# A four-layer decoder trunk on one core: x and result in whole quarters, a reordered norm chain, and eight weight parts split ahead of a layer

## The chip, the cores and the metric

The kernel runs on one core of one Trainium2 chip. The metric is the device time of one execution in microseconds; the median of several runs is given. Beside the runs there is one profiled execution with its trace. TensorE is PE in the profile, VectorE is DVE, ScalarE is ACT, GpSimd is POOL and SyncE is SP.

## The reference

256 tokens of 1024 values pass through four residual layers, and then one last RMSNorm. Layers 0 and 3 are a causal pooling mixer, layer 1 is a gated DeltaNet, layer 2 is latent attention. All is float32.

```python
def rmsnorm(x, g):
    xf = x.astype(jnp.float32)
    y = xf * lax.rsqrt(jnp.mean(xf * xf, axis=-1, keepdims=True) + EPS)
    return (y * g.astype(jnp.float32)).astype(x.dtype)

def reference(x, ...):
    for i in range(DEPTH):
        kind, j = i % N_MIXERS, i // N_MIXERS
        h = rmsnorm(x, norm_g[i])
        if kind == 0:
            y = pool_mixer(h, ...)
        elif kind == 1:
            y = gdn_mixer(h, ...)
        else:
            y = mla_mixer(h, ...)
        x = x + y.astype(x.dtype)
    return rmsnorm(x, final_g)
```

Every mixer is one wide input projection of `h`, work inside the mixer, and one output projection back to 1024 values.

## The kernel before, in words

**Layout.** The 256 tokens are two tiles of 128 partitions (`xs[0]`, `xs[1]`, called tile 0 and tile 1). Partition b*64 + a holds token 2a + b of its tile: `by_row` writes the DRAM side as a view with the order b, a, c. A tile is loaded and stored in quarters: quarter (t, c) is tile t, columns 512c to 512c + 511. Each `xs` tile has one extra column, `D`.

**Products in three parts.** A float32 product is made of three passes. Each operand is split into a high part, rounded to the matmul format (`hi`), and the rest (`lo`). For a weight, ACT casts `hi` (tile `whi`, line 149 or 153) and DVE, for some parts POOL, subtracts to get `lo` (tile `wlo`, line 150 or 154). A weight part is 128 rows of 512 columns; `weights` loads two parts (a unit) with one transfer on SP's queue into a `raw` buffer, and splits both. The split parts live in a ring of nine buffers each. A strip is 512 output columns, that is eight parts where the input has 1024 values.

**A layer's end.** `layer_out` makes the output projection in two strips of 512 columns. The second strip holds its last three units (six parts) back and then finishes the four pieces (tile 0 or 1, 256 columns each) in turn. `done` adds each piece to x on DVE (line 450) and calls `part_done`, which keeps a running sum of squares: ACT sums the squares (`sumsq`, line 256), POOL adds it to what came before. After the third quarter of the columns POOL puts a square root into the extra column of x (lines 297 and 298), so that the last sum of squares, over 257 columns, already holds the earlier ones. POOL then raises it to the power -1/2 (`xr`, line 390). `Normed.begin` multiplies 256 columns by the gain ahead of time on POOL (`hg`, line 385), and `rest` makes the two halves of the normed `h`: 256 columns of each on DVE (line 397), 256 on ACT from `hg` (line 402). PE transposes `h` (line 417) and ACT and DVE split it (lines 242 and 247) into `hT`, with which the next layer's first strip begins (line 162 for all weight matmuls).

**Order.** Each engine runs its instructions in one fixed order, which a scheduler writes from its own model of time when the kernel is built. `later(...)` tells it to keep an instruction behind a given one of the same engine. `held_back` uses this at the seam between two layers: the first `FREE` weight parts of the next layer may be split whenever the scheduler likes, and all further ones go behind the split of tile 0's `hT`:

```python
            held = held_back["free"] <= 0
            held_back["free"] -= 1
            with later(*(held_back["after"] if held else ())):
```

**Beginning and end.** At the start the quarters of x are loaded on SP's queue between the first weights (`load_x`, line 307; two transfers of 64 partitions per quarter). At the end `Final.feed` norms a tile and stores it with four transfers of 64 partitions on SP's queue (line 442). The tile pool `s4` holds the larger tiles of all layers (4 KB per partition each).

## Time and profile before

| | |
|---|---|
| median of the runs | 828.32 us (827.48 to 829.5, 3 runs) |
| profiled execution | 832.1 us, its span 830.4 us |
| granted TensorE clock | 0.986 of full speed, mean |
| PE, PEld busy | 96%, 91% of the span |
| DVE, ACT, POOL busy | 73%, 59%, 19% |
| transfers | 139.90 MB, mean 168 GB/s |

Times in the views count from the first instruction. A row of the timeline gives the start, the length, the engine, the line, the operation with output and inputs, and in square brackets how long the engine was idle before it and which instruction ended that idle time. PEld is the weight load of a matmul, which runs beside matmuls.

### The profile page before, as it was taken

What the parts mean: (1) busy time and instruction counts of PE and PEld (TensorE: products, weight loads), DVE (VectorE), ACT (ScalarE), POOL (GpSimd) and SP (SyncE); (2) the same over time, 40 slices, a digit from 0 to 9 for tenths busy, and PEclk for the clock granted to TensorE, in tenths of its full rate; (3) what the DMA queues carried; (4) which work ended last, traced back from release to release, by engine and by line L of the source; (5) the groups of instructions that cost most, each with busy time, mean ns of one, the idle gap of its engine ahead of it and who ended that gap; (6) DMA issues with size and microseconds to landing.
All of it is one profiled execution on the core that took longest, in us unless ns stands there. A gap on an engine that the chain in (4) does not pass through costs nothing.

```text
span 830.4 us, 16162 instructions
## 1 busy us (share of the span) xinstructions
PE 799.4 (96%) x5966; PEld 758.0 (91%) x5966; DVE 603.4 (73%) x1141; ACT 492.9 (59%) x993; POOL 159.8 (19%) x296
## 2 busy tenths in 40 slices
PE   8989999999898979999999999999999999999996
PEld 7989988989898978788989999999999989999996
DVE  4699887666987967356666678778877767877772
ACT  6665565567855655255566564666665565566662
POOL 2001100334236992023121112000000120000012
PEclk9999999999999989899999999999999999999998
DMA  6865666756655544303647786653552547576662
GB/s 204 224 180 167 193 209 210 221 153 195 193 135 180 163 139 118 124 12 115 187 125 224 231 180 185 192 164 102 153 175 80 179 143 214 183 223 202 202 204 51
DMA packets 109079, 139.90 MB, mean 168 GB/s; under 512 B 21316, under 2 KB 51208, under 8 KB 109000
## 3 DMA queue, kind: packets, MB, share of 16 engines
q1 hardware_dynamic: 106608, 137.12, 55.0%
q0 software_dynamic: 528, 1.58, 0.6%
q8 instruction: 47, 0.77, 0.4%
q10 hardware_dynamic: 1864, 0.17, 0.2%
q14 instruction: 32, 0.26, 0.1%
HBM read 137.27 MB, written 1.58 MB: 167 GB/s over the span
## 4 chain that ended last, share of the span: by engine, by line
PE 67%; DVE 11%; POOL 8%; DMA 8%; issue 4%; ACT 2%; SPq 0%; POOLq 0%; DVEq 0%; ACTq 0%
PE acc L162 53%; PE aux L162 7%; POOL pr L846 3%; DVE wlo L154 3%; POOL Tb L850 2%; DMA raw<-in_pool_w_out_dram 2%; DVE wlo L150 1%; DMA raw<-in_pool_w_in_dram 1%; DVE win L551 1%; DMA T<-d_t 1%; DMA Lb<-d_l 1%; DVE h L397 1%; DMA Gb<-d_g 1%; PE aux L979 1%; PE tp L1314 1%
## 5 line engine op out<-in xcount | busy, mean ns | idle before, releaser
L150 DVE TENSOR_TENSOR wlo<-raw,whi 128x512 fp32r<-128x512 f32 (+1 forms) x366 | 254.2, 719 | 104.3 <-ACT whi L149 100.8
L149 ACT CAST whi<-raw 128x512 fp32r<-128x512 f32 (+1 forms) x380 | 223.7, 617 | 167.6 <-PE acc L162 82.3
L162 PE MATMUL acc<-hTh,whi 128*128 128x256 f32 x832 | 230.7, 278 | 2.3 <-ACT gsg L670 1.5
L162 PE MATMUL acc<-hTl,whi 128*128 128x256 f32 x832 | 231.2, 278 | 0.0
L162 PE MATMUL acc<-hTh,wlo 128*128 128x256 f32 x832 | 229.8, 277 | 0.0
L162 PEld LDWEIGHTS acc<-hTh,whi 128*128 128x128 f32 x832 | 160.7, 193 | 2.9 <-ACT gsg L670 1.7
L162 PEld LDWEIGHTS acc<-hTl,whi 128*128 128x128 f32 x832 | 160.8, 193 | 0.3
L162 PEld LDWEIGHTS acc<-hTh,wlo 128*128 128x128 f32 x832 | 160.7, 193 | 0.1
L162 PE MATMUL acc<-wlo,yTh 128*128 128x256 f32 (+1 forms) x384 | 112.7, 312 | 0.8 <-DVE wlo L154 0.8
L162 PE MATMUL acc<-whi,yTh 128*128 128x256 f32 (+1 forms) x384 | 112.3, 315 | 0.0
L162 PE MATMUL acc<-whi,yTl 128*128 128x256 f32 (+1 forms) x384 | 89.1, 313 | 0.0
L162 PEld LDWEIGHTS acc<-wlo,yTh 128*128 128x128 f32 x384 | 73.2, 191 | 4.8 <-DVE wlo L154 1.7
L162 PEld LDWEIGHTS acc<-whi,yTh 128*128 128x128 f32 x384 | 72.9, 191 | 3.1
L162 PEld LDWEIGHTS acc<-whi,yTl 128*128 128x128 f32 x384 | 63.1, 191 | 3.4
L154 DVE SCALAR_TENSOR_TENSOR wlo<-raw,colsT,whi 128x512 fp32r<-128x512 f32 x64 | 47.0, 769 | 21.1 <-ACT whi L153 20.7
L153 ACT ACTIVATE whi<-raw,gain 128x512 fp32r<-128x512 f32 x64 | 43.6, 720 | 31.1 <-DMA raw<-in_pool_w_in_dram 22.6
L153 ACT ACTIVATE whi<-raw,colsT 128x512 fp32r<-128x512 f32 x64 | 43.5, 720 | 30.9 <-DMA raw<-in_pool_w_out_dram 18.0
L385 POOL TENSOR_TENSOR hg<-x,gain 128x256 f32<-128x256 f32 x16 | 13.4, 850 | 244.1 <-DVE x L450 244.1
L162 PE MATMUL acc<-wlo,hTh 128*128 128x512 f32 (+1 forms) x144 | 54.8, 385 | 1.9 <-DVE wlo L150 1.3
L154 DVE SCALAR_TENSOR_TENSOR wlo<-raw,gain,whi 128x512 fp32r<-128x512 f32 x64 | 46.6, 748 | 11.1 <-ACT whi L153 11.1
L162 PE MATMUL acc<-whi,hTh 128*128 128x512 f32 (+1 forms) x144 | 52.7, 379 | 0.7 <-ACT hTh L242 0.7
L162 PE MATMUL acc<-whi,hTl 128*128 128x512 f32 (+1 forms) x144 | 42.5, 373 | 0.0
(364 smaller groups left out, 1530.9 us busy)
## 6 DMA issues: line engine op xcount, KB each, us to landing
raw<-in_pool_w_in_dram SPq DMA_DIRECT2D x62, 512.0 KB, 4.4
raw<-in_gdn_w_in_dram SPq DMA_DIRECT2D x48, 512.0 KB, 4.0
raw<-in_pool_w_out_dram SPq DMA_DIRECT2D x32, 512.0 KB, 4.4
raw<-in_mla_w_in_dram SPq DMA_DIRECT2D x24, 512.0 KB, 4.5
raw<-in_mla_w_uq_dram SPq DMA_DIRECT2D x36, 256.0 KB, 3.4
raw<-in_pool_w_grp_dram SPq DMA_DIRECT2D x16, 512.0 KB, 3.8
raw<-in_gdn_w_out_dram SPq DMA_DIRECT2D x16, 512.0 KB, 3.8
raw<-in_mla_w_ukv_dram SPq DMA_DIRECT2D x32, 256.0 KB, 3.3
```

What stands on the lines that cost most here:

```text
L149: a = nc.scalar.copy(hi, v)
L150: b = e.tensor_tensor(out=lo, in0=v, in1=hi.bitcast(F32), op=ALU.subtract)
L153: a = nc.scalar.activation(hi, v, AF.Copy, scale=g)
L154: b = e.scalar_tensor_tensor(out=lo, in0=v, scalar=g, in1=hi.bitcast(F32), op0=ALU.mult, op1=ALU.subtract)
L162: return nc.tensor.matmul(inorder(o, n), lhsT=lhs, rhs=woven(rhs, n), start=start, stop=stop)
L385: nc.gpsimd.tensor_tensor(out=self.early[t, a], in0=xs[t][:, sl], in1=self.g[:, sl], op=ALU.mult)
L397: nc.vector.scalar_tensor_tensor(out=h[:, cut:], in0=xs[t][:, sl], scalar=r[:, 0:1], in1=self.g[:, sl], op0=ALU.mult, op1=ALU.mult)
L551: nc.vector.tensor_tensor(out=nxt[:, :, d:], in0=cur[:, :, d:], in1=cur[:, :, :S - d], op=ALU.add)
L846: nc.gpsimd.tensor_tensor(out=pv, op=ALU.mult, in0=Lb[:, r, r + 1:, None].to_broadcast([M * Q, n, c]), in1=Tb[:, r:r + 1, :c].to_broadcast ...
L850: mark["blocks"] = nc.gpsimd.tensor_tensor(out=tv, in0=tv, in1=pv, op=ALU.subtract).ins
L979: nc.tensor.matmul(ps[:, c], lhsT=U[0][:, h, :], rhs=vR[h // 2][:, 0, c * DV:(c + 1) * DV], start=True, stop=True)
L1314: nc.tensor.transpose(ps[:, a * P:(a + 1) * P], sb[:, a * P:(a + 1) * P], ident)
```

## The change

Four edits.

1. `load_x` and `Final.feed` move a quarter with one transfer instead of two. The last quarter of tile 1 is stored from ACT's queue.
2. `part_done` leaves out the division by `D` for the first three pieces of columns, so that POOL's multiplication ahead of the square root falls away; the small constant is scaled to fit.
3. `begin` for the columns from 512 on, which was free to run earlier on POOL, goes behind the square root (`mark["sofar"]`).
4. `FREE` is 8 instead of 4. Of the eight parts, the first four take ring buffers and the last four (`SPARE`) take a tile `wx` each from the pool `s4`, which holds high and low part together.

```diff
-    FREE = 4
+    FREE = 8
+    SPARE = 4
...
-            lo = ring.tile([P, CW], F32R, tag="wlo", name="wlo")[:, :cols]
-            hi = ring.tile([P, CW], F32R, tag="whi", name="whi")[:, :cols]
+            if 0 < held_back["free"] <= SPARE:
+                both = big("wx", 2, CW, dt=F32R)
+                hi, lo = both[:, 0, :cols], both[:, 1, :cols]
+            else:
+                lo = ring.tile([P, CW], F32R, tag="wlo", name="wlo")[:, :cols]
+                hi = ring.tile([P, CW], F32R, tag="whi", name="whi")[:, :cols]
...
+        unit = 1.0 / D if end or apart else 1.0
         with later(*[m for e, m in mark.items() if e == "rest"]):
-            sumsq(xs[t][:, a:a + n + more], n + more, s, scale=float(D) ** -0.5)
+            sumsq(xs[t][:, a:a + n + more], n + more, s, scale=unit ** 0.5)
         if a == 0:
-            nc.gpsimd.tensor_scalar(s, s, EPS, None, ALU.add)
+            nc.gpsimd.tensor_scalar(s, s, EPS * D * unit, None, ALU.add)
...
         if a and not end:
-            nc.gpsimd.tensor_scalar(s, s, float(D), None, ALU.mult)
-            nc.gpsimd.tensor_tensor(out=xs[t][:, D:], in0=s, in1=half, op=ALU.pow)
+            mark["sofar"] = nc.gpsimd.tensor_tensor(out=xs[t][:, D:], in0=s, in1=half,
+                                                    op=ALU.pow).ins
...
-        for b in range(2):
-            nc.sync.dma_start(out=xs[t][b * 64:(b + 1) * 64, sl], in_=by_row(x, t)[b, :, sl])
+        nc.sync.dma_start(out=xs[t][:, sl], in_=by_row(x, t)[:, :, sl])
...
-                for b in range(2):
-                    nc.sync.dma_start(out=by_row(out, t)[b, :, sl],
-                                      in_=y[c][b * 64:(b + 1) * 64])
+                queue = nc.scalar if c and t == NT - 1 else nc.sync
+                queue.dma_start(out=by_row(out, t)[:, :, sl], in_=y[c])
...
             if c == 0:
-                nxt.begin(t, CW)
+                with later(mark.pop("sofar")):
+                    nxt.begin(t, CW)
```

## The prediction

> **What bounds the kernel now.** I read the page's busy times first, then the chain of work that ended last, then the timeline at the start, at each seam between two layers, and at the end.

> ```profile
> span 830.4 us, 16162 instructions
> PE 799.4 (96%) x5966; PEld 758.0 (91%) x5966; DVE 603.4 (73%) x1141; ACT 492.9 (59%) x993; POOL 159.8 (19%) x296
> PE 67%; DVE 11%; POOL 8%; DMA 8%; issue 4%; ACT 2%; SPq 0%; POOLq 0%; DVEq 0%; ACTq 0%
> ```

> TensorE is busy for 96% of the span and carries 67% of the chain. The change touches none of its matmuls, so it can only win the idle time of PE (31 us in all) in the places that it touches, and the stretches before PE starts and after it ends. Those places are the loads of x, the three seams where a layer's last strip meets the next layer's first strip, and the tail. At the seams PE's own rows say what it waits for:

> ```profile
> 172.49 0.48 PE L162 MATMUL acc<-wlo,hTh 128*128 128x512 f32 x1 [0.65 <-POOL wlo L150]
> 173.38 0.48 PE L162 MATMUL acc<-wlo,hTh 128*128 128x512 f32 x1 [0.18 <-DVE wlo L150]
> 423.38 0.48 PE L162 MATMUL acc<-whi,hTh 128*128 128x512 f32 x1 [0.24 <-ACT hTh L242]
> 427.02 0.48 PE L162 MATMUL acc<-wlo,hTh 128*128 128x512 f32 x1 [0.57 <-DVE wlo L150]
> 674.53 0.48 PE L162 MATMUL acc<-wlo,hTh 128*128 128x512 f32 x1 [0.53 <-DVE wlo L150]
> 423.20:430.00 6.80, 6.05 (x31) 5.02 (x32) 5.78 (x10) 5.60 (x13) 1.03 (x2) 1.00 0.46 117
> ```

> The bracket is PE's idle time before the instruction and its releaser. Four waits are for the low part of a weight (wlo), 0.65 + 0.18 + 0.57 + 0.53 = 1.93 us. In the window row (length, then busy PE, PEld, DVE, ACT, POOL, granted clock, DMA share, GB/s) PE misses 6.80 - 6.05 = 0.75 us, nearly the 0.57 alone; the clock is 1.00, so nothing is throttled.

> **The eight parts.** Before, four of a strip's eight parts may be split ahead of token tile 0's norm; the fifth is held behind it. ACT and DVE around the second seam:

> ```profile
> 418.29 0.42 DVE L450 TENSOR_TENSOR x<-acc,x 128x256 f32<-128x256 f32 x1 [1.59 <-PE acc L162]
> 418.82 0.42 ACT L256 ACTIVATE junk<-x 128x257 f32<-128x257 f32 x1 [1.52 <-DVE x L450]
> 420.01 0.91 ACT L402 ACTIVATE h<-hg,xr 128x256 f32<-128x256 f32 x2 [0.68 <-POOL xr L390]
> 424.60 2.17 ACT L149 CAST whi<-raw 128x512 fp32r<-128x512 f32 x4
> 426.28 3.09 DVE L150 TENSOR_TENSOR wlo<-raw,whi 128x512 fp32r<-128x512 f32 x5
> 412.85 0.37 SPq L133 DMA_DIRECT2D raw<-in_mla_w_in_dram  x1
> 415.52 0.37 SPq L133 DMA_DIRECT2D raw<-in_mla_w_in_dram  x1
> DMA to landing us min/median/max: 4.5/4.6/4.9
> ```

> Parts 5 to 8 are the four casts at 424.60 and the subtractions from 426.28: PE, at wlo of part 5, waits to 427.02. Their raw data is there before: 412.85 + 4.6 = 417.5 for parts 5 and 6, 415.52 + 4.6 = 420.1 for 7 and 8. Freed from the hold, a part costs ACT 2.17/4 = 0.54 and DVE 3.09/5 = 0.62 us. ACT is idle for 1.52 us before 418.82, of it 1.3 after 417.5, where parts 5 and 6 fit (1.08), and parts 7 and 8 fit from 421 on, after `h`. Their raw buffers come free sooner too, and with them SP's next weight load, behind which nothing else is queued. All four are then ready before PE asks. The new tiles (wx) hold high and low part together, so the nine ring buffers, which the last strip's six held parts fill, are not needed. I take all 1.93 us; bounds 0 (the wx tiles come free only after the old strip, and everything stays as it is) and 2.4 (with the remaining 0.24 of two seams). What is late next: PE reaches token tile 1 0.6 us sooner, but the same four casts no longer stand ahead of tile 1's `h`, so that is ready some 2 us sooner. The 0.24 us for hTh stays, since it is PE's own transposes and ACT's cast. No row shows the wait for a wx buffer; its bad end is a rival below.

> **The shorter norm chain.** Each layer's second half loses one GpSimd multiply per token tile, and the product `hg` goes behind the power that fills the extra column of x. Tile 1 of the tail:

> ```profile
> 821.64 0.73 POOL L385 TENSOR_TENSOR hg<-x,gain 128x256 f32<-128x256 f32 x1 [1.39 <-DVE x L450]
> 822.34 0.19 POOL L294 TENSOR_TENSOR ms<-ms,ms 128x1 f32<-128x1 f32 x1
> 822.62 0.23 POOL L297 TENSOR_SCALAR ms<-ms 128x1 f32<-128x1 f32 x1
> 822.93 0.56 POOL L298 TENSOR_TENSOR x<-ms,half 128x1 f32<-128x1 f32 x1
> 824.11 0.55 POOL L390 TENSOR_TENSOR xr<-ms,neghalf 128x1 f32<-128x1 f32 x1 [0.62 <-ACT junk L256]
> 821.92 0.19 ACT L256 ACTIVATION_READ_ACCUMULATOR junk<-x 128x1 f32 x1
> 823.52 0.42 ACT L256 ACTIVATE junk<-x 128x257 f32<-128x257 f32 x1 [1.42 <-POOL x L298]
> 822.59 0.42 DVE L450 TENSOR_TENSOR x<-acc,x 128x256 f32<-128x256 f32 x1 [1.09 <-PE acc L162]
> ```

> The last square sum starts at 823.52 and waits for the power. Without `hg` ahead, the addition can follow the accumulator read (822.11) at 822.19; without the multiply the power starts 0.28 later, at 822.47, and ends at 823.03. Now DVE's addition (end 823.01) is the last, and with the 0.12 us that the same step takes at tile 0 (418.29 + 0.42 = 418.71 to 418.82, rows above) the sum starts at 823.12: 0.40 sooner. But `hg` now runs 823.09 to 823.82 on GpSimd, ahead of `xr`, which could have started at 823.71: `xr` starts at about 823.85, 0.26 sooner than 824.11. At the inner seams I cost the shorter chain at nothing. At the second one, the sum of tile 0 was released by DVE already (the 418.82 row), and `h` (420.01 + 0.91 = 420.92) lies ready until PE comes to its transposes:

> ```profile
> 422.11 1.04 PE L417 MATMUL tp<-ident,h 128*128 128x128 f32 x8
> ```

> That is 1.19 us of cover; if it were gone each microsecond more would cost its full price. Tile 1's chain there is covered by tile 0's 24 matmuls.

> **One store per quarter, the last on ACT's queue.**

> ```profile
> 825.25 1.11 SPq L442 DMA_DIRECT2D out_dram<-h  x2
> 827.05 0.59 SPq L442 DMA_DIRECT2D out_dram<-h  x1
> 824.69 1.01 DVE L397 SCALAR_TENSOR_TENSOR h<-x,xr,gain 128x256 f32<-128x256 f32 x2 [1.67 <-POOL xr L390]
> 822.00:823.00 1.00, 0.56 (x5) 0.36 (x4) 0.41 (x1) 0.10 (x2) 0.83 (x4) 1.00 0.97 207
> 826.00:827.00 1.00, 0.00 (x0) 0.00 (x0) 0.00 (x0) 0.00 (x0) 0.00 (x0) 0.50 0.60 127
> 827.00:828.00 1.00, 0.00 (x0) 0.00 (x0) 0.00 (x0) 0.00 (x0) 0.00 (x0) 0.50 0.98 213
> 828.00:829.00 1.00, 0.00 (x0) 0.00 (x0) 0.00 (x0) 0.00 (x0) 0.00 (x0) 0.50 0.86 184
> ```

> SP issues four stores of 128 KB one after another; the last starts at 827.05 although `h` is whole at 825.70. With two queues the second quarter goes out at about 825.44, 1.6 us sooner, and nothing stands behind it on ACT. But the data rows sum to 0.60 + 0.98 + 0.86 = 2.44 us at 210 GB/s from about 826.4, with the 16 engines at 0.98. If the engines set that rate, only the 0.26 of the chain arrives at the end. If SP's cadence set it (128 KB each 0.6 us is about the same rate), the data may go at the 322 GB/s of the loads (rows below): 1.6 us instead of 2.44, and the tail wins about 0.26 + 0.8 = 1.1. The share of 0.98 is nearer the first; I take 0.5, chain included, bounds 0.2 and 1.1.

> **One load per quarter.**

> ```profile
> 0.80 1.23 SPq L307 DMA_DIRECT2D x<-in_x_dram  x2
> 2.70 1.11 SPq L307 DMA_DIRECT2D x<-in_x_dram  x2
> 3.22 4.28 DMA x<-in_x_dram
> 7.63 1.09 PE L359 MATMUL tp<-ident,x 128*128 128x128 f32 x4 [1.37 <-DMA x<-in_x_dram]
> 0.00:5.00 5.00, 3.38 (x15) 3.10 (x16) 0.33 (x2) 1.49 (x2) 4.20 (x54) 1.00 0.48 135
> 5.00:10.00 5.00, 3.63 (x14) 3.09 (x14) 2.49 (x4) 3.08 (x7) 0.43 (x2) 1.00 0.87 252
> 10.00:15.00 5.00, 5.00 (x23) 4.27 (x23) 2.34 (x4) 2.43 (x5) 0.24 (x1) 1.00 1.01 322
> ```

> Four of eight issues of about 0.55 us go, and the weights between them move up as well. The second half of x(1,0) was issued at 3.22 and landed at 7.50, and PE waited 1.37 us for it. With one issue of x(0,0) and one of a weight ahead of it (0.80 + 2 x 0.6) it is issued at about 2.0, and with the same 4.28 it lands 1.2 us sooner. Against that, the engines' share is 0.87 and then 1.01: transfers begun sooner meet full engines. Bounds 0 and 1.4 (the wait, or 1.2 with a little of the later loads); I take the middle, 0.7.

> On how a transfer is spread, the rows say: stores of 64 rows hold the 16 engines at 0.97. A merged quarter has 128 rows on the chip's side, but its DRAM side is written as two groups of 64 rows, and no row here has an outer count of two. [...]

> **Sum.** Seams 1.93, start 0.7, tail 0.5: 3.1 us. The profiled execution took 832.1 (span 830.4, 1.7 around it), 3.8 above the median 828.32 of the runs (827.48 to 829.5), and would be 829.0; the median becomes 828.32 - 3.1 = 825.2. About 0.3% (2.5 us) is what a measurement of this kernel can tell from no change.

> **Rivals.** *Two engines, slower.* If a merged quarter is dealt out over its two groups, two engines move 256 KB. A store engine moves 207 / (0.97 x 16) = 13.3 GB/s, a load engine 322 / (1.01 x 16) = 19.9. The four stores (1.05 MB) on the same two engines take 26 to 39 us from 822 instead of ending at 828.9: 19 to 32 late. Four loads take 6.6 us each, the last landing near 28, while PE today has no gap from 10 on; the work on the columns that came first covers a little, so I count some 15 late. That gives 862 to 875, with one mechanism. It decides from about 8 engines down: there the last 512 KB take 4.9 instead of 2.44 us, and with the loads slowed as well the gain is gone. For it: the DRAM pattern's outer count. Against it: every transfer shown, 64 rows too, fills the engines. Chance 0.17.

> *The DMA merges are hidden, and wx opens part of the seams.* The share near 1.0 at start and end speaks for it, the open room on ACT against it: seams 1.0, tail 0.26, start 0.2, about 826.9. Chance 0.30, same.

> *A wx buffer is late.* If a cast into wx stands ahead of the 418.82 square sum on ACT and waits for the old strip's end (422.11), the chain is 3.3 late, 2.1 beyond its cover, at each of three seams: 6.3 more, less 1.2 at both ends: 833.4. Against it: the first strip's three ring parts wait for nothing today. Chance 0.04.

> **Numbers.** The forecast case has 0.49 (821 to 825.8, its bounds added: 3.1 + 0.47 + 0.6 + 0.7 = 4.9 would be 823.4, and below that only what reordered splits may add). The range 821.2 to 831.0 holds the forecast and the hidden case, 0.79, and the late buffer where it strikes one seam only; the two-engine case is left out. Faster 0.49, same 0.29, slower 0.22 (two engines 0.17, late buffers and their like 0.05).

> **What would show it.** Right: PE rows at the seams without a bracket for wlo; casts of parts 5 to 8 before 421 at the second seam; two stores at the tail, ACT's within 0.3 us of `h`, and data shares of 0.9 or more in about 2 us; the transposes of x(1,0) near 6.5, not 7.63. Wrong: DMA share near 0.12 (2 of 16) after the last `h`, x landing after 10, ACT casts released late by PE with the square sum behind them, or new waits on GpSimd's `xr` for `hg`.

## The result and the profile after

The changed kernel takes 868.25 us (median of 4 runs, 867.67 to 870.81), the kernel before beside it 828.91 (4 runs). The ratio is 1.0475, 95% interval [1.0436, 1.0513]: 4.8% slower. The profiled execution has a span of 865.9 us beside 830.4, at a mean granted clock of 0.974 beside 0.986. All prices below are from profiled executions, one per kernel.

The page's totals after:

```profile
span 865.9 us, 16110 instructions
PE 803.1 (93%) x5966; PEld 760.8 (88%) x5966; DVE 602.1 (70%) x1141; ACT 492.7 (57%) x993; POOL 160.0 (18%) x288
```

TensorE does the same work (803 us beside 799) in 35 us more. So the loss is idle time, and PE's list of waits (what waited, for what: us, times, longest) names it, first after, then before:

```profile
PE tp L364 <- DMA x<-in_x_dram: 15.7, 4, 5.1
PE aux L943 <- DMA T<-d_t: 9.7, 1, 9.7
```

```profile
PE tp L793 <- ACT kqT L787: 7.6, 4, 4.7
PE tp L359 <- DMA x<-in_x_dram: 1.9, 2, 1.4
```

PE now waits 15.7 us for x, and 9.7 us for a tile `T` in layer 1 for which it did not wait before. The start after, in the timelines of SP's queue and of PE:

```profile
0.80 0.70 SPq L312 DMA_DIRECT2D x<-in_x_dram  x1
2.02 0.56 SPq L312 DMA_DIRECT2D x<-in_x_dram  x1
8.89 1.12 PE L364 MATMUL tp<-ident,x 128*128 128x128 f32 x4 [5.07 <-DMA x<-in_x_dram]
15.23 1.12 PE L364 MATMUL tp<-ident,x 128*128 128x128 f32 x4 [4.38 <-DMA x<-in_x_dram]
21.27 1.11 PE L364 MATMUL tp<-ident,x 128*128 128x128 f32 x4 [4.49 <-DMA x<-in_x_dram]
```

The second quarter is issued at 2.02 and used only at 15.23. The first three quarters become usable about 6.2 us apart, and 262 KB in 6.2 us are 42 GB/s. The tail after, and two stretches, one of the start and one of the tail (length, busy PE, PEld, DVE, ACT, POOL, granted clock, DMA share, GB/s):

```profile
841.53 9.24 SPq L447 DMA_DIRECT2D out_dram<-h  x3
843.28 0.43 DVE L454 TENSOR_TENSOR x<-acc,x 128x256 f32<-128x256 f32 x1 [1.09 <-PE acc L167]
843.82 0.42 ACT L261 ACTIVATE junk<-x 128x257 f32<-128x257 f32 x1 [1.03 <-DVE x L454]
844.41 0.55 POOL L395 TENSOR_TENSOR xr<-ms,neghalf 128x1 f32<-128x1 f32 x1
849.67 0.51 ACT L407 ACTIVATE h<-hg,xr 128x256 f32<-128x256 f32 x1 [5.33 <-DMA out_dram<-h]
854.73 0.51 ACT L407 ACTIVATE h<-hg,xr 128x256 f32<-128x256 f32 x1 [4.55 <-DMA out_dram<-h]
855.40 0.65 ACTq L447 DMA_DIRECT2D out_dram<-h  x1
```

```profile
9.00:11.00 2.00, 1.86 (x8) 1.56 (x8) 0.34 (x1) 0.96 (x2) 0.00 (x0) 1.00 0.13 51
846.00:848.00 2.00, 0.00 (x0) 0.00 (x0) 0.00 (x0) 0.00 (x0) 0.00 (x0) 1.00 0.13 51
```

A DMA share of 0.13 is that of 2 busy engines of 16 (0.13 x 16 = 2.1). They move 51 GB/s, where the stores before moved 207 to 213. From the last addition (843.28) to the end pass 22.6 us, before 830.4 - 822.59 = 7.8. Tile 1's `h` cannot even be written: it has two buffers, and both are still being stored for tile 0 (the 5.33 and 4.55 us behind stores). That puts the last store out at 855.40, and it ends at 865.9.

The additions to x on DVE are good milestones (start of the first addition of each layer's output, and of its last one):

| layer's end | before | after | late |
|---|---|---|---|
| layer 0, first addition | 148.52 | 164.16 | 15.6 |
| layer 0, last | 168.46 | 184.06 | 15.6 |
| layer 1, first | 403.00 | 420.35 | 17.4 |
| layer 1, last | 422.58 | 439.65 | 17.1 |
| layer 2, first | 656.53 | 671.40 | 14.9 |
| layer 2, last | 670.12 | 689.17 | 19.1 |
| layer 3, last | 822.59 | 843.28 | 20.7 |
| end of the span | 830.4 | 865.9 | 35.5 |

So 15.6 us are lost at the start, 14.8 at the end, and 5.1 between, most of it at the third seam. Layer 1 loses 1.8 in spite of its 9.7 us wait, and layer 2 gives 2.2 back.

### The profile page after: what moved, and what is told of

It is laid out like the page before. It is cut to its first block, busy times and chain, and to the rows that moved or that the text cites. A ratio compares the mean times of both kernels' runs of the same rounds, so it can differ in the third digit from the quotient of the medians.

```text
span 865.9 us, 16110 instructions
## 1 busy us (share of the span) xinstructions
PE 803.1 (93%) x5966; PEld 760.8 (88%) x5966; DVE 602.1 (70%) x1141; ACT 492.7 (57%) x993; POOL 160.0 (18%) x288
## 4 chain that ended last, share of the span: by engine, by line
PE 73%; DMA 9%; POOL 6%; DVE 4%; ACT 2%; issue 2%; SPq 1%; ACTq 0%; DVEq 0%; POOLq 0%
PE acc L167 59%; PE aux L167 7%; POOL Tb L855 3%; POOL pr L851 2%; DMA x<-in_x_dram 2%; DMA raw<-in_pool_w_in_dram 2%; DMA out_dram<-h 1%; SPq L134 1%; DMA Gb<-d_g 1%; PE aux L943 1%; DMA raw<-in_pool_w_out_dram 1%; DVE wlo L159 1%; PE tp L1319 1%; DMA T<-d_t 1%; DMA Lb<-d_l 1%
## 5 line engine op out<-in xcount | busy, mean ns | idle before, releaser
L154 ACT CAST whi<-raw 128x512 fp32r<-128x512 f32 (+1 forms) x368 | 217.0, 617 | 177.3 <-PE acc L167 87.5
L155 DVE TENSOR_TENSOR wlo<-raw,whi 128x512 fp32r<-128x512 f32 (+1 forms) x355 | 244.4, 714 | 95.0 <-ACT whi L154 92.2
L390 POOL TENSOR_TENSOR hg<-x,gain 128x256 f32<-128x256 f32 x16 | 13.6, 860 | 208.0 <-DVE x L454 208.0
L167 PE MATMUL acc<-whi,hTh 128*128 128x512 f32 (+1 forms) x120 | 46.1, 393 | 1.2 <-ACT hTh L247 1.2
L167 PE MATMUL acc<-wlo,hTh 128*128 128x512 f32 (+1 forms) x120 | 46.6, 392 | 0.0
L167 PE MATMUL acc<-whi,hTl 128*128 128x512 f32 (+1 forms) x120 | 36.9, 383 | 0.0
```

The costliest lines, as they stand in the source:

```text
L154: a = nc.scalar.copy(hi, v)
L155: b = e.tensor_tensor(out=lo, in0=v, in1=hi.bitcast(F32), op=ALU.subtract)
L167: return nc.tensor.matmul(inorder(o, n), lhsT=lhs, rhs=woven(rhs, n), start=start, stop=stop)
L390: nc.gpsimd.tensor_tensor(out=self.early[t, a], in0=xs[t][:, sl], in1=self.g[:, sl], op=ALU.mult)
```

## The experiments

### Which edit costs what

Four kernels. `e1_loads` and `e2_stores` are the kernel before with one half of edit 1:

```diff
# e1_loads: load_x as in the change, all else as before
-        for b in range(2):
-            nc.sync.dma_start(out=xs[t][b * 64:(b + 1) * 64, sl], in_=by_row(x, t)[b, :, sl])
+        nc.sync.dma_start(out=xs[t][:, sl], in_=by_row(x, t)[:, :, sl])
# e2_stores: Final.feed as in the change, all else as before
# e3_rest: the change, with load_x and Final.feed as before
# e4_g16: the change, with 16 groups
-        return a[0, t * P:(t + 1) * P, :].rearrange("(a b) c -> b a c", b=2)
+        return a[0, t * P:(t + 1) * P, :].rearrange("(a b) c -> b a c", b=16)
```

> The kernel before with one change: a quarter of x is loaded with one transfer. Theory (two engines carry a transfer whose DRAM side has two groups): every load takes about 6.3 us at 2/16 of the engines, the first strip of the first layer ends some 15.6 us later as in the changed kernel, time about 844. Rival (the loads hide behind the weights, the loss comes from elsewhere): within 2 us of 829.

> The kernel before with one change: a quarter of the result is stored with one transfer, the last one from ACT's queue. Theory (two engines): a store takes about 5 us on them, tile 1's h waits for tile 0's stores because h has two buffers, the tail from the last addition to the end grows by about 14.8 us, time about 843.5. Rival (only the issue order at the end counts): 828 to 829.

> The changed kernel with the loads and stores in two transfers per quarter again, so only the norm chain and the eight parts are left. The changed trace lost 35.5 us of span, of it 15.6 by the first strip's end and 14.8 in the tail. Theory A (the other 5.1 us are a cost of the eight parts and the order that they make, most of it at the third seam): about 833 to 834. Theory B (the other 5.1 us are late effects of the slow loads; the seams win the 1.9 us predicted): 826 to 827.

> The changed kernel with the 128 tokens of a tile in sixteen groups of 8 rows on the DRAM side instead of two groups of 64; the number, size and order of all transfers and instructions are the same (tokens are put to other partitions, which changes what the causal layers compute, not the work). Theory (the outer count sets the number of engines): 16 engines carry a quarter, x is whole by about 8 us, the tail is at most 10 us from the last h of tile 0, time 826 to 834, whatever the rest of the change costs. Rival (one transfer of 128 rows is slow as such, or the order of the queue is at fault): 865 to 870 as the changed kernel.

| kernel | median us | ratio to before (830.59) |
|---|---|---|
| e1_loads | 844.3 | 1.0177 [1.0150, 1.0204] |
| e2_stores | 847.37 | 1.0200 [1.0184, 1.0216] |
| e3_rest | 836.25 | 1.0071 [1.0052, 1.0089] |
| e4_g16 | 836.49 | 1.0072 [1.0049, 1.0095] |

1.0177 x 1.0200 x 1.0071 = 1.0455, within the interval of the whole change: three losses that add up. (The build of `e1_loads` also puts some of the first strip's matmuls in another order.) In `e1_loads` PE waits for x as it does after, and the first addition of layer 0 comes 13.2 us late (161.74); in `e2_stores` the way from the last addition (822.29) to the end is 22.9 us. With 16 groups both losses are gone, and `e4_g16` equals `e3_rest`. PE's wait for x in `e1_loads`, and two stretches of `e4_g16` that hold stores:

```profile
PE tp L358 <- DMA x<-in_x_dram: 15.8, 4, 5.2
```

```profile
829.00:830.00 1.00, 0.05 (x1) 0.00 (x0) 0.42 (x1) 0.37 (x2) 1.00 (x2) 1.00 0.97 301
833.00:834.00 1.00, 0.00 (x0) 0.00 (x0) 0.00 (x0) 0.00 (x0) 0.00 (x0) 0.73 0.96 305
```

Same transfers, same number of bytes, same written order on the engines: only the outer count of the DRAM pattern (its number of groups) went from 2 to 16, and the share from 0.13 to 0.97. What I had not foreseen stands in the third row of the table: edits 2 to 4 alone cost 0.7%. Neither theory of `e3_rest` has its time; Theory A is the nearer, some 2 us short.

### The count of groups as a dose

As with 16 groups, another count also changes which token lies in which partition, and so what the layers compute, but no work of any engine.

```diff
-        return a[0, t * P:(t + 1) * P, :].rearrange("(a b) c -> b a c", b=2)
+        return a[0, t * P:(t + 1) * P, :].rearrange("(a b) c -> b a c", b=4)   # e8_g8: b=8
```

> As e4, with four groups of 32 rows on the DRAM side. Theory (as many engines as groups): DMA share 0.25 while stores alone run, about 100 GB/s, a quarter of x in about 3.2 us and a store in 2.5 us; time between e4 (836.5) and the changed kernel (868), near 841. Rival (two groups are a special case): as e4 or as the changed kernel.

> As e4, with eight groups of 16 rows on the DRAM side. Theory (as many engines as groups): DMA share 0.5 while stores alone run, about 200 GB/s; time within 2 us of e4 (836.5), since the cover of the weights is back. Rival: as e7.

Stretches with stores alone, of `e7_g4` and of `e8_g8`, and the first wait of tile 1's `h` in each:

```profile
845.00:846.00 1.00, 0.00 (x0) 0.00 (x0) 0.00 (x0) 0.00 (x0) 0.00 (x0) 0.50 0.26 102
840.06 0.51 ACT L407 ACTIVATE h<-hg,xr 128x256 f32<-128x256 f32 x1 [3.44 <-DMA out_dram<-h]
```

```profile
838.00:839.00 1.00, 0.00 (x0) 0.00 (x0) 0.00 (x0) 0.00 (x0) 0.00 (x0) 0.50 0.49 123
834.23 0.51 ACT L407 ACTIVATE h<-hg,xr 128x256 f32<-128x256 f32 x1 [1.44 <-DMA out_dram<-h]
```

2, 4, 8 and 16 groups hold 0.13, 0.26, 0.49 and 0.97 of the engines, and the kernels take 868.25, 853.38, 843.56 and 836.49 us (single executions for 4 and 8). Both took longer than I expected: `e7_g4` near 841 us, `e8_g8` within 2 us of 836.5. In the tail of `e7_g4` tile 1's `h` waits 3.44 and then 1.99 us for buffers that are still being stored, and from the last addition (835.57) to the end pass 16.0 us.

Times 16 the four shares are 2.1, 4.2, 7.8 and 15.5: in these four runs about as many engines are busy as there are groups.

### Edits 2 to 4: work or order

`e3_rest` has less work on GpSimd than before, yet PE waits for `T` in it. `T` is the end of a chain on GpSimd and a round trip through DRAM in the middle of layer 1. I split the rest into the eight parts and the norm chain:

```diff
# e5_free8: the kernel before with edit 4 (FREE = 8, wx)
# e6_chain: the kernel before with edits 2 and 3 (no multiplication by D, hg behind the power)
```

> The kernel before with FREE = 8 and the wx tiles alone; loads, stores and norm chain as before. The kernel with both this and the new norm chain (e3) loses 0.7%, 5.4 us of it in layer 1 (PE waits 12.5 us for the transfer T<-d_t, which it did not wait for before) and 4.6 us at the third seam. Theory A (the eight parts make the scheduler write another order for the engines, and that order costs both): 834 to 838, with the wait for T<-d_t of over 8 us and the third seam some 4 us longer. Theory B (the moved hg and the shorter chain make that order, the eight parts win their 1.9 us): 828 to 830.

> The kernel before with the shorter norm chain and hg behind the square root alone; FREE = 4, loads and stores as before. Theory A of e5: the tail is 0.3 to 0.4 us shorter, the rest as before, 830 to 831 on this chip. Theory B of e5: 834 to 837, with the long wait for T<-d_t and the longer third seam.

`e5_free8` took 839.68, ratio 1.0096 [1.0068, 1.0124], and `e6_chain` 837.0, ratio 1.0076 [1.0052, 1.0101], beside 830.41. Each alone costs at least what both cost together, so neither theory holds as it stands: the loss belongs to no one edit. Both show the long wait of PE; `e5_free8`, then `e6_chain`:

```profile
PE aux L943 <- DMA T<-d_t: 12.1, 1, 12.1
```

```profile
PE aux L940 <- DMA T<-d_t: 10.2, 1, 10.2
```

So I compared the orders that the scheduler writes. The chain edit made in layer 0, 1 or 3 leaves the order of PE, ACT and DVE as it was, instruction for instruction. Made in layer 2 alone, it gives another matmul to 469 of the 5754 places in PE's order, the same ones as in `e6_chain`: 312 of them in layer 1, which ends 250 us ahead of the edited place, and 141 at the end of layer 2. The orders of `e5_free8` and of `e3_rest` have the same matmuls in all these places. (The build also puts some tiles at other places in memory; no run separates that from the order.) Layer 2's work has not begun when layer 1 runs, so this kernel tells order from work:

```diff
# e9_chain_l2 (the kernel before with the chain edit in layer 2 only)
+            if not short:
+                nc.gpsimd.tensor_scalar(s, s, float(D), None, ALU.mult)
...
-            part_done(t, a, n)
+            part_done(t, a, n, short=i == 2)
...
-                nxt.begin(t, CW)
+                with later(*([mark["sofar"]] if i == 2 else [])):
+                    nxt.begin(t, CW)
```

> The kernel before with the shorter norm chain and the later product hg in layer 2 alone (the third seam); the other layers keep the old chain, and all transfers are as before. Two multiplications of 0.23 us fall away on GpSimd. Built, this program has another written order on PE, ACT and DVE than the kernel before, most of it inside layer 1, which runs some 250 us ahead of the edited place; the same edit in any other layer leaves that order as it was. Theory O (the order that the scheduler writes costs the time, not the work of the edit): layer 1 shows the long wait of PE for T (10 to 12.5 us, not 5 or less), the x addition that ends layer 1's first strip comes 3 to 5 us late, the third seam loses a further 2 to 3, and the time is 834 to 838 beside 830. Rival C (the chain edit itself, or the other place of hg on GpSimd, holds the seams back): only the third seam is touched, layer 1 keeps its times to 0.5 us, and the time is 829 to 833.

It took 838.43, ratio 1.0083 [1.0054, 1.0112], as Theory O has it, a little beyond its 838. The first addition at the end of layer 1 comes at 408.70, before 403.00: from the last addition of layer 0 that is 239.1 us beside 234.5. Around the wait, `e9_chain_l2` and below it the kernel before (timeline of PE, then the same 15 us of each, then the stretch from the first matmul on `T` to the end of the layer's first output strip):

```profile
315.73 3.65 PE L942 MATMUL aux<-T,LT 128*128 128x64 f32 x16 [11.27 <-DMA T<-d_t]
300.00:315.00 15.00, 4.46 (x28) 3.76 (x27) 2.72 (x8) 2.78 (x7) 14.18 (x25) 0.75 0.35 104
315.70:408.70 93.00, 91.28 (x497) 80.00 (x498) 52.09 (x101) 42.67 (x105) 14.70 (x36) 0.92 0.27 92
319.40:323.00 3.60, 3.60 (x9) 2.87 (x10) 3.60 (x9) 0.00 (x0) 0.00 (x0) 0.50 0.28 74
```

```profile
313.73 1.89 PE L938 MATMUL aux<-T,LT 128*128 128x64 f32 x16
300.00:315.00 15.00, 14.17 (x94) 13.82 (x95) 8.63 (x19) 9.36 (x19) 14.35 (x22) 0.81 0.48 132
313.70:403.00 89.30, 87.29 (x498) 76.39 (x498) 52.29 (x101) 43.48 (x107) 13.89 (x36) 0.96 0.29 95
```

GpSimd is equally busy in both (14.18 and 14.35 of 15 us), since it works on the chain that ends in `T`. Before, PE has 14.17 us of other work left in that stretch; in the new order it has done that work earlier, has 4.46 us left, and then sits idle.

The long wait itself is the smaller part of the price. From the last addition of layer 0 to the first matmul on `T` it takes 315.73 - 169.60 = 146.1 us, before 313.73 - 168.46 = 145.3: 0.9 us more. The other 3.7 of the 4.6 us come behind it. There PE is busy for 91.28 us instead of 87.29 with the same matmuls, at a mean granted clock of 0.92 instead of 0.96: after the 11 us of idle time the clock is still at 0.50 (the row at 319.40), and the 16 matmuls on `T` take 3.65 us instead of 1.89.

The third seam loses too: from its first addition to its last pass 677.98 - 660.58 = 17.4 us, before 13.6, a little more than the 2 to 3 us that Theory O had. Three of its four additions wait on DVE behind weight splits that wait for late weights:

```profile
669.35 1.14 ACT L149 CAST whi<-raw 128x512 fp32r<-128x512 f32 x2 [1.35 <-DMA raw<-in_mla_w_out_dram]
670.00 2.62 DVE L150 TENSOR_TENSOR wlo<-raw,whi 128x512 fp32r<-128x512 f32 x4 [1.20 <-ACT whi L149]
673.97 1.08 DVE L453 TENSOR_TENSOR x<-acc,x 128x256 f32<-128x256 f32 x3
```

For layer 1 it is thereby shown that what the scheduler writes costs the time, and not the work of the edit. For the third seam it is the likely one: the edit itself stands there. `e5_free8` has no chain edit but the same order of PE there, and needs 680.95 - 661.30 = 19.7 us; but it has the eight parts at that seam, and no run has the order alone.

### What the edits are worth where the order stays

```diff
# e10_wx_l1: the kernel before with eight free parts and wx for layer 1 alone
+                held_back.update(free=FREE if self.i in (1,) else 4, after=ins,
+                                 wx=self.i in (1,))
# e11_chain_rest_actq: the chain edit in every layer but layer 2; two transfers per
# quarter, the last quarter's two on ACT's queue
+            part_done(t, a, n, short=i != 2)
...
+                queue = nc.scalar if c and t == NT - 1 else nc.sync
                 for b in range(2):
-                    nc.sync.dma_start(out=by_row(out, t)[b, :, sl],
+                    queue.dma_start(out=by_row(out, t)[b, :, sl],
# e12_best: both
```

> The kernel before with eight free parts and the wx tiles for layer 1 alone (the first seam), everything else as before. The order of PE differs only around that seam. Theory O: the eight parts do open this seam where the order stays otherwise: PE's two waits there for a low part, 0.83 us, go, layer 1 and the third seam run as before, and the time is 829.3 to 830.2 beside 830.3. Rival F (a free part stands ahead of tile 0's norm on ACT or DVE, or the wx tile comes late): the waits stay or others come in their place, and the time is 830.3 to 833.

> The kernel before with the shorter chain and the later hg in every layer but layer 2, two transfers of 64 rows for each quarter as before, and the last quarter's two on ACT's queue. The order of PE and DVE is that of the kernel before, instruction for instruction. Theory O: no loss anywhere; the last square sum is released by the addition on DVE and xr comes 0.26 to 0.4 us sooner, the ACT queue issues the last quarter 1 to 1.6 us sooner while the 16 engines are full: 829.3 to 830.1 beside 830.3, the tail from the last addition 7.0 to 7.5 instead of 7.8. Rival C (the chain edit costs where it stands): three of its four places are edited here, so 833 to 837.

> The last kernel with the eight free parts for layer 1 as well: everything of the change that leaves the order of layers 1 to 3 as it was. Theory O: the gains add up, 0.5 to 0.8 for the first seam and 0.3 to 0.7 for the tail: 828.8 to 829.8 beside 830.3. Rivals C and F: their losses add up, 833 to 840.

| kernel | median us | ratio to before (831.15) |
|---|---|---|
| e10_wx_l1 | 831.65 | 1.0015 [0.9993, 1.0038] |
| e11_chain_rest_actq | 828.2 | 0.9964 [0.9947, 0.9981] |
| e12_best | 831.1 | 0.9997 [0.9975, 1.0020] |

`e11_chain_rest_actq` beats both kernels. The eight parts gain nothing (`e10_wx_l1`), and added to `e11` they seem to take its gain back, though the two intervals overlap a little: against the forecast of `e12_best`, the gains do not add up. `e10_wx_l1` went as Rival F has it. At the first seam PE's waits of `e10_wx_l1`, with the casts on ACT and the subtractions on DVE and GpSimd:

```profile
168.63 0.91 ACT L407 ACTIVATE h<-hg,xr 128x256 f32<-128x256 f32 x2 [0.19 <-POOL xr L395]
169.44 2.16 ACT L154 CAST wx<-raw 128x512 fp32r<-128x512 f32 x4
170.60 3.63 DVE L155 TENSOR_TENSOR wx<-raw,wx 128x512 fp32r<-128x512 f32 x3 [0.49 <-ACT wx L154]
171.46 1.03 PE L167 MATMUL acc<-wx,hTh 128*128 128x512 f32 x3 [0.38 <-POOL wx L155]
174.29 0.48 PE L167 MATMUL acc<-wx,hTh 128*128 128x512 f32 x1 [0.72 <-DVE wx L155]
```

The parts are free of the hold, but the scheduler now writes their four casts behind the last `h` of tile 1, where before they stood ahead of it, and PE waits 0.38 + 0.72 us where it waited 0.65 + 0.18 before. The three subtractions on DVE take 3.63 us, where three took 1.88 before (at 172.64): GpSimd subtracts beside them (1.28 us from 170.12, 1.48 from 172.21). In `e11_chain_rest_actq` the hold is as before (four free parts), and PE's only wait in the same stretch is

```profile
PE acc L162 <- ACT hTh L242: 0.2, 1, 0.2
```

The wait for `wlo` is gone there without any part having been freed. The reason stands on GpSimd. The first seam before, then in `e11_chain_rest_actq`:

```profile
167.25 0.74 POOL L385 TENSOR_TENSOR hg<-x,gain 128x256 f32<-128x256 f32 x1 [1.38 <-DVE x L450]
167.35 1.18 DVE L150 TENSOR_TENSOR wlo<-raw,whi 128x512 fp32r<-128x512 f32 x1 [0.24 <-ACT whi L149]
167.50 1.04 PE L417 MATMUL tp<-ident,h 128*128 128x128 f32 x8
167.94 0.64 POOL L294 TENSOR_TENSOR ms<-ms,ms 128x1 f32<-128x1 f32 x1
169.58 0.42 ACT L256 ACTIVATE junk<-x 128x257 f32<-128x257 f32 x1 [0.85 <-POOL x L298]
170.46 2.18 ACT L149 CAST whi<-raw 128x512 fp32r<-128x512 f32 x4
```

```profile
164.99 0.69 DVE L150 TENSOR_TENSOR wlo<-raw,whi 128x512 fp32r<-128x512 f32 x1 [0.29 <-ACT whi L149]
165.45 0.28 POOL L295 TENSOR_TENSOR ms<-ms,ms 128x1 f32<-128x1 f32 x1 [2.00 <-ACT junk L256]
165.59 1.04 PE L420 MATMUL tp<-ident,h 128*128 128x128 f32 x8
166.32 0.72 POOL L388 TENSOR_TENSOR hg<-x,gain 128x256 f32<-128x256 f32 x1
166.71 0.43 ACT L256 ACTIVATE junk<-x 128x257 f32<-128x257 f32 x1
167.59 2.18 ACT L149 CAST whi<-raw 128x512 fp32r<-128x512 f32 x4
```

In both, ACT makes the casts of parts 5 to 8 behind tile 1's last square sum (128x257). Before, that sum waits 0.85 us for GpSimd's power, which stands behind `hg`, the addition and the multiplication, and the casts start 170.46 - 167.50 = 2.96 us after PE's transposes of tile 0. In `e11_chain_rest_actq` the sum waits for nothing, and they start 167.59 - 165.59 = 2.00 us after. PE, DVE and ACT have the same order of work in both.

Part of the old chain's length came about between two engines. Before, `hg` and a subtraction on DVE start together; the subtraction takes 1.18 us instead of 0.69, and GpSimd's small addition behind `hg` 0.64 instead of 0.19 or 0.28. With `hg` moved behind the power they no longer meet. How much of the gain is due to this and how much to the multiplication of 0.23 us that is gone, no run separates. The tail of `e11_chain_rest_actq` is 826.4 - 819.23 = 7.2 us, before 7.8:

```profile
819.23 0.42 DVE L454 TENSOR_TENSOR x<-acc,x 128x256 f32<-128x256 f32 x1 [1.09 <-PE acc L162]
822.44 1.20 ACTq L446 DMA_DIRECT2D out_dram<-h  x2
```

The waits for `wlo` at the first two seams (0.65 + 0.18 + 0.57), less 0.3 more at the third, and 0.6 of the tail make about 1.7 us, at the lower end of the measured 1.6 to 4.4. The two spans differ by 4.0, of which 2.6 lie ahead of layer 0's first addition (145.93 beside 148.52), where nothing was edited, so that part is a difference between executions.

## Why the prediction was wrong, point by point

- **One load and one store per quarter: the step that failed.** I bounded the load by 0 and 1.4 us of gain and the store by 0.2 and 1.1, and left out of the sum the one thing that the pattern itself showed, its outer count of two. The reason given against it, that every transfer shown fills the engines, proved nothing: each of those had an outer count of 64 or 128. With an outer count of two the share was 0.13, two engines of 16 for a quarter, and the cost was 13.2 us for the loads and 15.1 for the stores.
- **The rival "two engines, slower"** is what happened, with a chance of 0.17. That two groups would mean two engines was shown by no row of before; the shares of 0.13 at the start and in the tail after show it. That 868 lies within its 862 to 875 is partly luck: loads and stores alone make 1.0177 x 1.0200 = 1.038, that is 860 beside 828.9, and edits 2 to 4 added the rest. The rival had the loads right: 19.9 GB/s an engine forecast, 42 / 2 = 21 of x's data measured (25.5 with the weights in the same stretch), "some 15 late" and 15.6 found (13.2 with the loads alone). The stores, forecast 19 to 32 late and found 15.1, were mis-sized in two ways that partly cancel: an engine moves 51 / 2 = 25.5 GB/s, not 13.3, but the wait of tile 1's `h` for its buffers was not seen. 13.3 was no property of an engine; it was the rate that 128 KB pieces reached on 16 of them. Its point of break-even held: with 8 groups the kernel is 7 us slower than with 16.
- **The eight parts, 1.93 us at the seams.** The waits were read rightly, their cause wrongly. I put them down to the hold, and the room on ACT to early casts. Where the parts were freed, the scheduler did not use that room. The waits came from tile 1's chain on GpSimd, which I had called covered by tile 0's 24 matmuls: the casts for those very matmuls stand behind its last square sum, and with the shorter chain the waits at the first two seams went.
- **The shorter chain.** Right where it was costed. From the last addition to `xr` it takes 844.41 - 843.28 = 1.13 us after and 1.52 before, 0.39 sooner against 0.26 forecast, and the last square sum is released by DVE as said. Costing it at nothing at the inner seams was wrong: that is where most of what can be told of `e11_chain_rest_actq`'s gain lies. I had read tile 0's square sum at the second seam, which DVE released; the one that counted was tile 1's, which GpSimd's power released.
- **The rival "DMA merges are hidden"** holds once all 16 engines serve a merged quarter: `e4_g16` equals `e3_rest`, which has two transfers. Its tail is 835.9 - 829.09 = 6.8 us, beside 7.4 in `e3_rest` and 7.8 before. So with 16 engines the tail wins 1.0 us, of it 0.6 by the stores; I had taken 0.5, chain included, with 1.1 as the bound. The runs' times do not resolve it.
- **Not in any case:** that a few instructions less in layer 2 make the scheduler rewrite layer 1, for 0.7 to 1.0%. I had costed the edits in a fixed order. The "late wx buffer" did not occur; no wait for a wx buffer shows. But the argument against it, that the parts split early wait for nothing, was misread: the cast at 414.15 before waits 1.10 us for PE, though its raw data had come with the part before it.

## What to carry to other kernels

## What the runs showed of the hardware that I had not expected

- Two or four engines moved more each than all sixteen: stores went at 25.5 GB/s an engine on 2 or 4 engines (51 and 102 GB/s), and at 303 / (0.965 x 16) = 19.6 on 16 with 256 KB transfers, but 13.3 with 128 KB transfers on 16 (207 GB/s at a share of 0.97). On 8 engines it was 123 / 8 = 15.4 in the stretch shown. Why the 128 KB transfers are slower than the 256 KB ones on 16 is open: they also cover 64 partitions instead of 128.
- DVE and GpSimd held each other up at the seams: before, at each of the three, a 128x512 subtraction on DVE that started 0.10 to 0.14 us behind `hg` took 1.14 to 1.18 us (at 167.35, 421.50 and 669.05), where others with no GpSimd instruction beside them took 0.66 to 0.69. The 128x1 addition behind `hg` on GpSimd then took 0.64 to 0.65 (at 167.94, 422.06 and 669.60), and 0.19 to 0.20 behind the other tile's `hg` and in the tail. Each of these subtractions ended 0.54 us after `hg`. What held them is not shown. Not every meeting did it: beside other GpSimd instructions such subtractions took from 0.67 to 1.77 us.
- A wait of TensorE in layer 1 cost more than its own length: in `e9_chain_l2` it ends at 315.73 after 11.27 us, the granted clock is 0.50 from 319.40 to 323.00, and 128x512 matmuls start 0.43 us apart up to 324.40, then 0.22 apart from 324.64 on. In the changed kernel, behind the wait of 9.7 us that ends at 329.5, the clock is 0.50 from 330 to 336 and 1.00 from 340 to 344; in the kernel before, behind 4.69 us that end at 300.83, it is 0.50 from 302 to 304 and 1.00 from 306 to 308.
